# The S5 input product of a hybrid mixer block, issued for two row bands at a time (QB = 1 to 2)

## The chip, the core and the metric

One core of one Trainium2 chip runs the whole program: TensorE (matmuls into PSUM), VectorE, ScalarE, GpSimd and SyncE, with DMA engines that load the weights. The metric is the device time of one execution in microseconds.

## The reference, cut to what matters

One layer over 256 tokens of width 2048: a mixer of three branches (gated delta rule, gated linear attention, S5 state space), then cross attention, then a convolutional feed-forward part. The change is in the S5 branch:

```python
def s5_ssm(u, lam_re, lam_im, log_step, b_re, b_im, c_re, c_im, d_skip):
    uf = u.astype(f32).reshape(bsz, s, S5_GROUPS, S5_GROUP)      # 64 groups of 16 features
    ...
    bbr = zr[..., None] * br - zi[..., None] * bi                # discretised input matrices
    bbi = zr[..., None] * bi + zi[..., None] * br
    bu_r = jnp.einsum('bsgh,gph->sbgp', uf, bbr)                 # the input product: 16 -> 64 a group
    bu_i = jnp.einsum('bsgh,gph->sbgp', uf, bbi)
    ...
    _, _, xr, xi = lax.associative_scan(combine, (a_r, a_i, bu_r, bu_i), axis=0)   # over 256 tokens
    y = (jnp.einsum('sbgp,ghp->bsgh', xr, c_re) - jnp.einsum('sbgp,ghp->bsgh', xi, c_im))
    ...
```

All of it is float32.

## The kernel before

**The large products.** Weights come in slabs of two k-tiles by 512 columns (`raw`, loaded through SyncE's queue). `load_w` (L206) splits each into a high part `whi` (ScalarE's cast) and a low part `wlo` (VectorE's subtraction). TensorE multiplies high and low parts in separate passes: `tile_passes` (L222 high, L226 low) where features come out on the partitions, `proj_tok` (L282, L286) where tokens do. Those passes use all 128 rows of the array. The order of high and low passes in `tile_passes` is the same in both kernels. Their sums stand in five PSUM tiles `acc`; the other three PSUM banks are a ring of tiles `mx` (L126), which every small product shares.

**Background work.** The three branches are generators. `proj` and `proj_tok` call `pump` after each slab, which lets each generator run for as much as its rate allows; a `yield` says what the step was worth. So the small products stand among the slabs' passes. A scheduler with a timeline of its own then orders the instructions of each engine; after that every engine works in that order.

**The S5 generator** (`s5_core`). For each half of the sequence (128 tokens) it fills `X`, the input product for all 64 groups, real and imaginary, with two groups of 64 states on the 128 partitions. The input `su` has 32 rows (two groups of 16 features) for each product, so a feature tile holds four row bands of 32, and `Bl` holds the matrices for the same rows. One step takes one band `q` and two feature tiles: four matmuls (L921: two feature tiles by real and imaginary) into one `mx` tile, each 32 rows by 128 weight columns by 128 tokens at `tile_position=(32 * q, 0)`, and then one copy of that tile to `X` on ScalarE (L925). There are 16 steps in a half. When the last is copied, the scan runs on VectorE, three small instructions for each token (L931 to L933), and then the output product (L946). The first half's steps stand among the passes of the delta rule's key slabs (L222, L226), where the key tiles are also transposed (L397); the second half's among the last gate and value slabs (L282, L286) and the first delta-rule output gate slabs (L222, L226). L593 is a product of the delta rule's state, in 64-row bands that alternate between two `mx` tiles; L602, L599 and L640 are others of it.

The constant `QB` sets how many bands one step takes. The loop is

```python
            for f2 in range(4):
                for q2 in range(0, 4, QB):
                    pss = [self.mx([P, 2, 2, P]) for _ in range(QB)]
                    for n in range(2):
                        ft = 2 * f2 + n
                        for c in range(2):
                            for q, ps in enumerate(pss, q2):
                                rs = slice(32 * q, 32 * q + 32)
                                nc.tensor.matmul(ps[:, n, c, :], self.Bl[c][rs, ft, :], su[rs, ft, tk], start=True,
                                                 stop=True, tile_position=(32 * q, 0))
                    for q, ps in enumerate(pss, q2):
                        p0 = 8 * f2 + q
                        nc.scalar.copy(X[:, :, p0:p0 + 5:4, :].rearrange("p c n s -> p n c s"), ps)
                    yield 1.0 * QB
```

Of the kernel before, what the change touches and what calls it, by code (L numbers as in the profile page):

```python
# [40 lines left out]
R_EB = 0.4  # L41
SP5 = 0
TAIL = 3
QB = 1
HPA = 0
R_N1 = 0.8
R_N2 = 1.3
# [41 lines left out]
class Net:  # L89
# [814 lines left out]
    def s5_core(self, ctr, cti):  # L904
# [5 lines left out]
        for hf in range(2):  # L910
            X = self.s5p.tile([P, 2, 32, P], F32, name="X", tag="X")
            tk = slice(hf * P, hf * P + P)
# [4 lines that stand above are left out]
# [6 lines left out]
# [4 lines that stand above are left out]
            for t in range(P):  # L927
# [645 lines left out]
```

## Time and profile before

| | |
|---|---|
| median of 3 runs | 1924.62 us (1921.52 to 1929.48) |
| the profiled execution | 1925.81 us |
| its span, first to last instruction | 1924.0 us |
| mean granted TensorE clock | 0.991 |
| DMA | 363.93 MB, mean 189 GB/s |

The profile gives each engine's busy time; the chain of work that ended last, which follows the last instruction back through whatever released it, and so tells which engine sets the end; and groups of instructions by line, with what ended the idle time ahead of them. In a group's row, `32*128 32x128` is a weight tile of 32 rows by 128 columns and 32 rows by 128 moved columns. "PEclk" in a table by stage is the clock granted to TensorE as a share of full speed. Matmuls are pipelined: the busy time of one overlaps the next, so that a mean duration is longer than the distance from one to the next.

### The profile page before, as it was taken

The page shows a single profiled execution, that of the slowest core. Times are in us where ns is not written, and L with a number is a line of the kernel's source. Part 1 is how long each engine was busy: PE and PEld are TensorE (multiplying, and loading weights), DVE is VectorE, ACT ScalarE, POOL GpSimd, SP SyncE. Part 2 cuts the span into 40 slices and gives each one's busy share as a digit, 9 for nine tenths or more (in the row PEclk, how much of TensorE's full clock was granted, in tenths as well). Part 3 has the DMA queues.
Part 4 walks back from the last instruction along what each step waited for, and adds up shares of the span by engine and source line. Part 5 has one row for each costly group of instructions (what it writes and reads, how often), then busy time and mean ns, then how long its engine had stood idle before and what let it go on. Part 6 is the DMA issues. An engine that isn't in the chain of part 4 may idle for free.

```text
span 1924.0 us, 28133 instructions
## 1 busy us (share of the span) xinstructions
PE 1873.0 (97%) x10440; PEld 1573.9 (82%) x10440; DVE 1415.4 (74%) x2719; ACT 959.6 (50%) x1428; POOL 67.4 (4%) x117
## 2 busy tenths in 40 slices
PE   7999999999999999999999997999999999999997
PEld 6788888777877688888888986888888888888886
DVE  6878999997469999977666755777666677644445
ACT  5655544443564444444455654655555555544442
POOL 0000012020000000000000000000000000000000
PEclk9989999999999999999999998999999999999999
DMA  7544477674445575666587544766666656766664
GB/s 256 164 130 155 155 210 234 195 253 140 133 121 162 182 225 177 213 216 216 186 266 225 174 153 140 219 182 184 201 188 188 189 183 186 228 215 198 198 195 131
DMA packets 107482, 363.93 MB, mean 189 GB/s; under 512 B 12320, under 2 KB 20896, under 8 KB 106832
## 3 DMA queue, kind: packets, MB, share of 16 engines
q1 hardware_dynamic: 97696, 328.32, 55.3%
q0 software_dynamic: 9648, 33.81, 5.3%
q8 instruction: 82, 1.34, 0.3%
q14 instruction: 56, 0.46, 0.1%
HBM read 350.47 MB, written 11.61 MB: 188 GB/s over the span
## 4 chain that ended last, share of the span: by engine, by line
PE 89%; DVE 6%; ACT 2%; issue 1%; DMA 1%; DVEq 0%; SPq 0%; POOL 0%; ACTq 0%; POOLq 0%
PE acc L282 28%; PE acc L222 27%; PE acc L286 14%; PE acc L226 14%; DVE wlo L206 2%; PE mx L921 2%; DMA raw<-in 1%; ACT whi L206 1%; DVE r L388 1%; PE mx L183 0%; PE mx L640 0%; DVE mm L931 0%; DVE f L518 0%; PE mx L946 0%; DVE X L933 0%
## 5 line engine op out<-in xcount | busy, mean ns | idle before, releaser
L206 DVE TENSOR_TENSOR wlo<-raw,whi 128x1024 fp32r<-128x1024 f32 (+1 forms) x632 | 752.3, 1195 | 388.3 <-ACT whi L206 366.6
L206 ACT CAST whi<-raw 128x1024 fp32r<-128x1024 f32 (+1 forms) x632 | 645.6, 1029 | 672.1 <-PE acc L282 339.1
L222 PE MATMUL acc<-aa,whi 128*128 128x512 f32 x2224 | 620.7, 398 | 10.7 <-DVE r L212 8.3
L222 PEld LDWEIGHTS acc<-aa,whi 128*128 128x128 f32 x2224 | 383.6, 190 | 63.9 <-issue 9.8
L226 PEld LDWEIGHTS acc<-aa,wlo 128*128 128x128 f32 x2224 | 345.4, 191 | 59.1 <-DVE wlo L206 11.5
L226 PE MATMUL acc<-aa,wlo 128*128 128x256 f32 x2224 | 362.1, 283 | 7.6 <-DVE wlo L206 7.4
L282 PE MATMUL acc<-whi,aa 128*128 128x512 f32 (+1 forms) x1408 | 346.5, 383 | 0.0
L282 PEld LDWEIGHTS acc<-whi,aa 128*128 128x128 f32 x1408 | 255.3, 188 | 53.3 <-issue 2.3
L286 PE MATMUL acc<-wlo,aa 128*128 128x512 f32 (+1 forms) x704 | 191.5, 383 | 2.8 <-DVE wlo L206 2.7
L286 PEld LDWEIGHTS acc<-wlo,aa 128*128 128x128 f32 x704 | 127.9, 188 | 31.5 <-DVE wlo L206 6.6
L282 PE MATMUL acc<-whi,ach 128*128 128x512 f32 x352 | 137.0, 389 | 0.0
L282 PE MATMUL acc<-whi,acl 128*128 128x512 f32 x352 | 136.9, 389 | 0.0
L931 DVE TENSOR_TENSOR mm<-M,X 128x128 f32<-128x128 f32 x254 | 98.7, 389 | 5.1 <-ACT X L925 0.3
L286 PE MATMUL acc<-wlo,ach 128*128 128x512 f32 x352 | 95.4, 389 | 0.0
L282 PEld LDWEIGHTS acc<-whi,ach 128*128 128x128 f32 x352 | 66.1, 188 | 13.7
L286 PEld LDWEIGHTS acc<-wlo,ach 128*128 128x128 f32 x352 | 66.1, 188 | 13.7
L282 PEld LDWEIGHTS acc<-whi,acl 128*128 128x128 f32 x352 | 66.0, 188 | 13.7
L933 DVE TENSOR_TENSOR X<-X,s__868 128x64 f32<-128x64 f32 x255 | 71.6, 281 | 4.8
L282 PE MATMUL acc<-whi,mgx 128*128 128x512 f32 x256 | 64.3, 391 | 0.1
L211 ACT COPY r<-acc 128x256 f32<-128x256 f32 x143 | 49.6, 362 | 27.3 <-PE acc L222 26.8
L932 DVE TENSOR_TENSOR s__868<-mm 128x64 f32<-128x64 f32 x255 | 56.5, 222 | 4.5
L212 DVE TENSOR_TENSOR r<-r,acc 128x256 f32<-128x256 f32 x143 | 57.0, 413 | 0.9 <-ACT r L211 0.9
(439 smaller groups left out, 1558.5 us busy)
## 6 DMA issues: line engine op xcount, KB each, us to landing
raw<-in SPq DMA_DIRECT2D x600, 512.0 KB, 4.0
raw<-in SPq DMA_DIRECT2D x32, 256.0 KB, 2.7
gd<-r POOLq DMA_DIRECT2D x24, 256.0 KB, 4.4
f<-gd POOLq DMA_DIRECT2D x12, 512.0 KB, 4.8
f<-Rd POOLq DMA_DIRECT2D x4, 512.0 KB, 7.2
f<-in POOLq DMA_DIRECT2D x4, 512.0 KB, 4.5
gp<-in POOLq DMA_DIRECT2D x8, 256.0 KB, 4.7
xn<-in POOLq DMA_DIRECT2D x1, 2048.0 KB, 11.0
```

The source lines that it names most:

```text
L206: self.last = (nc.scalar.copy(hi, raw), self.seq(lambda: nc.vector.tensor_sub(lo, raw, hi.bitcast(F32))))
L211: self.nc.scalar.copy(r, acc[:, T:2 * T])
L212: self.nc.vector.tensor_add(r, r, acc[:, 0:T])
L222: nc.tensor.matmul(accs[m], hi[:, kk, ms[m]], xs[kk].rearrange("p c s -> p (c s)"), start=ks[kk] == 0, stop=ks[kk] == KT - 1)
L226: nc.tensor.matmul(accs[m][:, :T], lo[:, kk, ms[m]], xs[kk][:, 0, :], start=False, stop=False)
L282: nc.tensor.matmul(accs[t], xs[kk][i][:, t * P:(t + 1) * P], hi[:, kk, :], start=ks[kk] == 0 and i == 0, stop=False)
L286: last[:] = [nc.tensor.matmul(accs[t], xs[kk][0][:, t * P:(t + 1) * P], lo[:, kk, :], start=False, stop=ks[kk] == KT - 1)]
L388: nc.vector.scalar_tensor_tensor(c[:, d:], raw[:, :T - d], w[:, j, 3 - d:4 - d], c[:, d:], op0=ALU.mult, op1=ALU.add)
L921: nc.tensor.matmul(ps[:, n, c, :], self.Bl[c][rs, ft, :], su[rs, ft, tk], start=True, stop=True, tile_position=(32 * q, 0))
L931: nc.vector.tensor_mul(m, self.M, prev[:, None].broadcast_to([P, 2, 2, 32]))
L932: nc.vector.tensor_add(s, m[:, :, 0, :], m[:, :, 1, :])
L933: nc.vector.tensor_add(X[:, :, :, t], X[:, :, :, t], s)
```

## The change

One constant:

```diff
-QB = 1
+QB = 2
```

One step of `s5_core` now takes two `mx` tiles and two bands. For each feature tile and each of the real and imaginary parts it issues the matmul of the one band and then that of the other, so that neighbours have different rows of the array and different PSUM tiles; then both tiles are copied, and the step counts 2.0 instead of 1.0. There are 8 steps in a half.

TensorE, second half, among the gate slabs. `mx_4924` is the step's PSUM tile, `bl0` and `bl1` are the real and imaginary matrices. Before:

```order
L286 MATMUL acc_4821<-wlo_4908,aa_448 128x512 x2
L921 MATMUL mx_4924<-f8_107,bl0_449 128x128
L921 MATMUL mx_4924<-f8_107,bl1_450 128x128
L921 MATMUL mx_4924<-f8_107,bl0_449 128x128
L921 MATMUL mx_4924<-f8_107,bl1_450 128x128
L282 MATMUL acc_4820<-whi_4931,aa_448 128x512 x4
L282 MATMUL acc_4821<-whi_4931,aa_448 128x512 x4
L286 MATMUL acc_4820<-wlo_4932,aa_448 128x512 x2
L286 MATMUL acc_4821<-wlo_4932,aa_448 128x512 x2
L921 MATMUL mx_4948<-f8_107,bl0_449 128x128
```

Now:

```order
L286 MATMUL acc_4821<-wlo_4908,aa_448 128x512 x2
L921 MATMUL mx_4924<-f8_107,bl0_449 128x128
L921 MATMUL mx_4925<-f8_107,bl0_449 128x128
L921 MATMUL mx_4924<-f8_107,bl1_450 128x128
L921 MATMUL mx_4925<-f8_107,bl1_450 128x128
```

The same four rows follow once more for the second feature tile, and then L282. What stood behind the next slab (`mx_4948`) is now the second tile here. Six of the eight steps of the second half read like this. The first two of it do not alternate throughout; the first, behind the output product of the first half:

```order
L946 MATMUL mx_4645<-X_869,f4_4468 32x128 x4
L921 MATMUL mx_4778<-f8_107,bl0_449 128x128
L921 MATMUL mx_4778<-f8_107,bl1_450 128x128
L921 MATMUL mx_4778<-f8_107,bl0_449 128x128
L921 MATMUL mx_4779<-f8_107,bl0_449 128x128
L921 MATMUL mx_4779<-f8_107,bl1_450 128x128
L921 MATMUL mx_4779<-f8_107,bl0_449 128x128
L921 MATMUL mx_4778<-f8_107,bl1_450 128x128
L921 MATMUL mx_4779<-f8_107,bl1_450 128x128
```

Three matmuls of one band are followed by three of the other, and then one of each. In the first half the steps stand closer, and the scheduler takes some of them apart. The second step there, `mx_926` and `mx_927`, now:

```order
L921 MATMUL mx_871<-f8_107,bl1_450 128x128
L921 MATMUL mx_926<-f8_107,bl0_449 128x128
L921 MATMUL mx_926<-f8_107,bl1_450 128x128
L921 MATMUL mx_926<-f8_107,bl0_449 128x128
L921 MATMUL mx_926<-f8_107,bl1_450 128x128
L226 MATMUL acc_1404<-aa_448,wlo_1466 128x256 x2
L222 MATMUL acc_1405<-aa_448,whi_1409 128x512 x2
```

`mx_926` stands behind the first pair (whose last matmul is the first row), and `mx_927` comes 14 large passes later, with the third pair right behind it. Two more pairs of the first half are taken apart in this way. By the order, the first half's 16 tiles stand in 10 places among the large passes before and in 8 now; the second half's in 15 before and in 8 now. In the first half, four more L222 matmuls stand ahead of the last tile's than before.

ScalarE, second half, copies of `X` among the weight casts. Before:

```order
L206 CAST whi_4973<-raw_4972 128x1024
L925 COPY X_4777<-mx_4924 128x2x2x128
L206 CAST whi_5003<-raw_5002 128x1024
L925 COPY X_4777<-mx_4948 128x2x2x128
L206 CAST whi_5027<-raw_5026 128x1024
```

Now:

```order
L206 CAST whi_4973<-raw_4972 128x1024
L925 COPY X_4777<-mx_4924 128x2x2x128
L925 COPY X_4777<-mx_4925 128x2x2x128
L206 CAST whi_5009<-raw_5008 128x1024
L206 CAST whi_5027<-raw_5026 128x1024
```

The two copies of a step now stand together, ahead of the casts. The order of the queues of SyncE and GpSimd is the same in both kernels.

## Prediction

> **What bounds the kernel now.** I read the page's busy lines first, then the chain of work that ended last, then the group of the line that is changed.
>
> ```profile
> PE 1873.0 (97%) x10440; PEld 1573.9 (82%) x10440; DVE 1415.4 (74%) x2719; ACT 959.6 (50%) x1428; POOL 67.4 (4%) x117
> PE 89%; DVE 6%; ACT 2%; issue 1%; DMA 1%; DVEq 0%; SPq 0%; POOL 0%; ACTq 0%; POOLq 0%
> PE acc L282 28%; PE acc L222 27%; PE acc L286 14%; PE acc L226 14%; DVE wlo L206 2%; PE mx L921 2%; DMA raw<-in 1%; ACT whi L206 1%; DVE r L388 1%; PE mx L183 0%; PE mx L640 0%; DVE mm L931 0%; DVE f L518 0%; PE mx L946 0%; DVE X L933 0%
> L921 PE MATMUL mx<-f,bl 32*128 32x128 f32 x256 | 35.6, 299 | 0.2 <-DVE bl L897 0.2
> ```
>
> TensorE is the bound: 89% of the chain. Line 921, the S5 input product, is 2% of it, so some 38 us at the very most. The program has 128 such matmuls and the trace 256 records: each fp32 matmul runs as two passes of 32 rows by 128 columns. The busy time is not the price, since passes overlap in it; the price has to be read from the chain in order of time, stage by stage. L921 stands in two stages, one for each half of the sequence:
>
> ```profile
> core 0: us, PE busy (x) PEld busy (x) DVE busy (x) ACT busy (x) POOL busy (x), PEclk, DMA share, GB/s
> 120.40:134.00 13.60, 13.60 (x54) 11.62 (x53) 6.84 (x24) 6.64 (x14) 0.00 (x0) 0.50 0.17 55
> 134.00:158.70 24.70, 24.70 (x169) 20.90 (x169) 13.59 (x38) 14.14 (x23) 0.00 (x0) 1.00 0.34 107
> 158.70:450.00 291.30, 283.55 (x1626) 232.86 (x1626) 281.81 (x646) 132.94 (x182) 32.01 (x55) 1.00 0.65 198
> 484.00:558.00 74.00, 74.00 (x401) 59.46 (x391) 36.33 (x56) 43.49 (x62) 0.53 (x1) 1.00 0.45 136
> 558.00:580.00 22.00, 17.43 (x151) 14.72 (x149) 22.00 (x37) 11.85 (x15) 0.00 (x0) 1.00 0.40 120
> ```
>
> In 120.4 to 158.7 (first half) and 484 to 558 (second half) TensorE is busy without a gap while VectorE has half its time free; DMA is far from full. What TensorE saves there moves the end of the stage. In the stages behind (158.7 to 450, 558 to 580) VectorE is the full engine: 281.8 of 291.3 us, and 22.0 of 22.0. They begin when the scan of L931 has the last X tile, so they begin earlier by what the loading stage saves, and don't shrink. The first row also shows 13.6 us at half the clock, at a place where L921 stands.
>
> **The price of a group now.** The chain in order of time, second half, and behind it three stretches from elsewhere (the first half's later groups, and L593):
>
> ```profile
> 484.60 1.82 PE mx L921 x15
> ...
> 493.10 2.04 PE acc L282 x8
> 495.13 0.91 PE acc L286 x4
> 496.04 1.81 PE acc L282 x8
> 497.85 0.91 PE acc L286 x4
> 498.76 1.08 PE mx L921 x8
> 499.84 2.04 PE acc L282 x8
> 501.88 0.91 PE acc L286 x4
> 502.78 1.08 PE mx L921 x8
> ```
>
> ```profile
> 135.65 2.19 PE mx L921 x24
> ...
> 139.91 1.08 PE mx L921 x8
> ...
> 153.93 1.64 PE mx L921 x16
> ...
> 428.12 1.09 PE mx L593 x16
> ```
>
> A lone group (4 matmuls, 8 passes, one row band) takes 1.08 us, and the eight L282 matmuls behind it take 2.04 instead of 1.81: 0.23 us for the switch between 32-row and full tiles. Where two or three groups of different bands happen to stand together, the next one adds only 1.64 − 1.08 = 0.56 (2.19 − 1.64 = 0.55): the bands already overlap, by a lookahead of a few passes. L593 is the nearest thing to what the change makes: fp32, 128 weight columns, 128 moved columns, two bands (of 64 rows) in turn, each with its own PSUM bank. Its 16 passes take 1.09 us, what 8 passes of one band take. So a pair whose bands alternate should take 1.09, against 2 × (1.08 + 0.23) apart or 1.64 + 0.23 side by side.
>
> **Second half, step by step.** Before: 15 clusters by the order, the first of two groups (1.82), then 14 lone ones: 1.82 + 14 × 1.08 + 15 × 0.23 = 20.4 us. After: 8 clusters. Six alternate at every matmul: 6 × 1.09. The first two go three matmuls of one band, three of the other, then one each; between 1.09 (full overlap) and 1.64 (only the lookahead) I take 1.4. Sum 6 × 1.09 + 2 × 1.4 + 8 × 0.23 = 11.2. Saved 9.2.
>
> **First half.** Before: 10 clusters of 24, 8, 8, 24, 8, 16, 8, 8, 16 and 8 passes, at full clock 2 × 2.19 + 6 × 1.08 + 2 × 1.64 + 10 × 0.23 = 16.4. After: 8 clusters, and not all pairs: three PSUM tiles are not enough for the density here, and the order tears three pairs apart. One is an alternating pair with a lone band behind it (1.09 + 0.56 = 1.65); two are a lone band, then a pair that alternates only in its second half (between 1.65 and 2.19, I take 1.8, nearer the overlapped end since all three bands differ); two are full pairs (1.09); three are lone (1.08). 1.65 + 2 × 1.8 + 2 × 1.09 + 3 × 1.08 + 8 × 0.23 = 12.5. Saved 3.9, of which 0.9 is lost again for the scan, because the order puts four more L222 matmuls (0.23 each, as 1.81 / 8 shows for the like L282) in front of the last lone band. Net 3.0. That some of these ran at half clock changes nothing as long as the half-clock stretch keeps its length: the work that is pushed out of it is then other work.
>
> **What else moves.** The X copies of L925 come two in a row on ScalarE, with the weight casts behind them by 0.6 us more:
>
> ```profile
> L925 ACT COPY X<-mx x32: 566/587/632, 120.4 to 559.3; 128x512 f32<-128x512 f32 x32
> PEld mx L921 <- ACT X L925: 0.2, 1, 0.2
> ```
>
> Two copies are 1.17 us. The casts feed three buffers and ScalarE is busy 43.5 of 74 us in the second half, so I cost this at nothing; if that cover went, TensorE would wait at the next L282. Each pair now holds two of the three mx tiles from its first matmul to the second copy. Before, TensorE waited 0.2 us for that in the whole first half. From below it costs 0, from above one copy, 0.59 us, at each of the 16 pairs, 9.4 us; I take 0, nearest the 0.2, since pairs of the second half stand at least 12 matmuls (2.7 us, 1.81 + 0.91) apart. SP's and POOL's queues keep their order; VectorE's rows around the scan change places within some 20 rows, with the same work in each stage.
>
> **Sum.** 9.2 + 3.0 = 12.2 us. The profiled execution took 1925.81 us (span 1924.0), 1.2 above the median of 1924.62; it goes to 1913.6, the median to 1912.4. I say 1912. About 0.5% (9.6 us) is what a measurement of this kernel tells from no change: the three runs shown lie 8 us apart.
>
> **A rule weighed.** Here is the pass-to-pass time, from one lone group shown whole and one cut by the window's edge after seven passes:
>
> ```profile
> 498.69 1.15 PE L921 MATMUL mx<-f,bl 32*128 32x128 f32 x8
> ...
> 502.71 1.04 PE L921 MATMUL mx<-f,bl 32*128 32x128 f32 x7
> ```
>
> One pass of a band takes 0.11 us, so a neighbouring group that adds 0.56 has three of its eight passes under the group before it. The Trainium skill (TensorE: Matmul & The Clock Gate, Part 3: Packing small matmuls — row/col tiling) says that row groups overlap, but that matmuls start and end strictly in program order. By strict order a group behind another could hide one pass alone and would add 0.77; the torn pairs would then cost about 1 us more in all, and the sum would be 11. The trace's 0.56 says that a later band does run ahead, so I keep my prices.
>
> **Rivals.**
> - The bands don't alternate, or not at this size: 32-row bands in turn gain no more than neighbours do. For it: no row shows 32-row bands that alternate by the matmul. Against: L593 and the 0.56. Pairs at 1.64 and the torn clusters at 2.19: second half 8 × 1.64 + 1.84 = 15.0, saved 5.4; first half 3 × 2.19 + 2 × 1.64 + 3 × 1.08 + 1.84 = 14.9, saved 1.5, net 0.6. Sum 6, time 1918.6.
> - VectorE takes back the first half. It is full from 158.7 to 450; if its stage there is tied to weights arriving and not to X, only the 9.2 of the second half stay: 1915.4. If the second half too is lost to the 22 us behind it (TensorE stands idle 4.6 there), up to that much again: 1920. For it: VectorE's full rows. Against: both stages open with work that waits for X.
> - The half-clock stretch changes. 13.6 us at 0.50 cost 6.8. With less 32-row work in it, it could end sooner; without it the time is 1912.4 − 6.8 = 1905.6, and a longer one costs half of what it adds. The Trainium skill (the same page, Part 1: The HAM clock gate) has the full clock back after one busy window of about 3.4 us; the row at 0.50 has TensorE busy for four such stretches, so the trace doesn't bear that out, and I can't foretell this length.
> - Slower: TensorE, which issues in order, stands at a pair's first matmul of the second band until ScalarE has freed its mx tile, with every accumulating matmul behind it. The price is ScalarE's place: a copy (0.59) behind a weight cast (1.03 mean) is 1.6 us. From 12.2 / 16 = 0.76 us a pair the gain is gone; with 1.6 at all 16 pairs, 25.9 − 12.2 = 13.7 is lost and the time is 1938. Against it: the 0.2 us. The Trainium skill (TensorEngine Tiling (Array Packing), PSUM Bottleneck) warns of this: tiling speeds TensorE, and the copies out of PSUM may become the bottleneck; copies of 1.17 for a pair of 1.09 would agree with it if pairs followed each other, which they do only in the first half.
>
> ```profile
> L206 ACT CAST whi<-raw 128x1024 fp32r<-128x1024 f32 (+1 forms) x632 | 645.6, 1029 | 672.1 <-PE acc L282 339.1
> ```
>
> **How the numbers follow.** The forecast (1908 to 1917 with its unknown prices) has 0.62; no alternation or VectorE taking part back (1915 to 1921) 0.22; the half-clock stretch shorter (1904 to 1909) 0.10; slower or unchanged by PSUM waits 0.06. The range 1905 to 1921 leaves out about 2 in 10. Faster than 1915.0: 0.54 of the first case and all of the third, 0.64. Within 0.5%: the rest of the first, the second, 0.02 of the last, 0.32. Slower: 0.04.
>
> **What would show it.** In the chain of the changed kernel, L921 pieces of 16 passes at about 1.09, eight clusters in the second half, and that half's loading stage 9 us shorter than 74. Pieces of 1.6 for a pair would show the alternation wrong; TensorE waiting for X of L925 by more than a few us would show the PSUM rival; a stage 158.7 to 450 that is longer by what was saved ahead of it, the VectorE one. A granted clock at half for longer or shorter than 13.6 us near 120 would be the third. It would be wrong altogether if the pairs fall apart on the chip, or if VectorE starts its scan no earlier.

## The result and the profile after

| | before | changed |
|---|---|---|
| median, first comparison | 1924.62 us (7 runs, 1921.52 to 1929.48) | 1915.03 us (7 runs, 1911.12 to 1919.79) |
| ratio | | 0.9944 [0.9932, 0.9956] |
| median, second comparison | 1923.43 us (16 runs) | 1911.23 us (6 runs) |
| ratio | | 0.9941 [0.9929, 0.9953] |
| profiled execution, span, granted clock | 1925.81, 1924.0, 0.991 | 1911.12, 1909.3, 0.994 |

The kernel became 0.56 to 0.59% faster, some 11 us, just past the 0.5% that can be told from no change. For the second comparison I had expected 1914 to 1916, and it came out 3 us lower. The page of the changed kernel (busy lines, the chain by engine and by line, the group of L921):

```profile
PE 1857.7 (97%) x10440; PEld 1561.2 (82%) x10440; DVE 1414.6 (74%) x2719; ACT 958.1 (50%) x1428; POOL 67.4 (4%) x117
PE 86%; DVE 8%; issue 2%; ACT 2%; DMA 1%; DVEq 0%; SPq 0%; POOL 0%; ACTq 0%; POOLq 0%
L921 PE MATMUL mx<-f,bl 32*128 32x128 f32 x256 | 21.3, 283 | 0.2 <-DVE bl L897 0.2
```

TensorE's busy time fell by 15.3 us, L921's by 14.3 (35.6 to 21.3), with the same 256 records. VectorE's share of the chain rose from 6 to 8%: the first sign that part of the saving met another path. The chain in order of time, first half, then second half:

```profile
123.90 1.65 PE mx L921 x23
128.75 1.08 PE mx L921 x8
132.12 1.65 PE mx L921 x23
137.48 1.09 PE mx L921 x16
143.10 1.09 PE mx L921 x16
145.81 1.08 PE mx L921 x8
148.01 1.08 PE mx L921 x8
```

```profile
474.38 1.82 PE mx L921 x16
480.32 1.42 PE mx L921 x16
487.67 1.09 PE mx L921 x16
488.76 2.04 PE acc L282 x8
490.79 0.91 PE acc L286 x4
...
497.14 1.09 PE mx L921 x16
503.89 1.09 PE mx L921 x16
513.37 1.09 PE mx L921 x16
522.84 1.09 PE mx L921 x16
```

A pair whose bands alternate takes 1.09 us, what one band takes alone, and the switch back to full tiles costs the same 0.23 (2.04 against 1.81). The stages, cut at the same instructions in both kernels. Before: from the start of the first half's products to the last X copy, from the second half's first L921 to the first L673, and from there to the first L640:

```profile
core 0: us, PE busy (x) PEld busy (x) DVE busy (x) ACT busy (x) POOL busy (x), PEclk, DMA share, GB/s
119.00:158.70 39.70, 39.54 (x234) 33.75 (x234) 21.83 (x63) 21.49 (x39) 0.00 (x0) 0.83 0.30 94
484.50:543.10 58.60, 58.60 (x298) 46.68 (x294) 26.41 (x43) 31.60 (x46) 0.53 (x1) 1.00 0.46 137
543.10:583.80 40.70, 35.76 (x245) 29.93 (x244) 35.08 (x60) 25.47 (x36) 0.00 (x0) 0.97 0.38 114
```

The same three in the changed kernel:

```profile
119.00:149.80 30.80, 30.50 (x238) 25.69 (x238) 21.76 (x63) 21.24 (x39) 0.00 (x0) 1.00 0.44 130
474.30:526.80 52.50, 52.50 (x306) 42.55 (x302) 26.52 (x43) 32.02 (x47) 0.53 (x1) 1.00 0.52 153
526.80:567.60 40.80, 36.36 (x239) 29.34 (x238) 34.30 (x58) 23.67 (x34) 0.00 (x0) 0.92 0.37 114
```

The first stage is 8.9 us shorter; 0.17 × 39.7 = 6.7 of that is clock, since the stretch at half speed is gone, and 2.2 is work. The second is 6.1 shorter at full clock. The third is as long as before; its lower clock (0.92 against 0.97) does not show in its length. The shift between the two traces is 10.2 us where the second half begins (484.5 to 474.3), 16.2 at L640 (583.8 to 567.6) and 14.7 at the end of the span. The 1.5 given back on the way differs from profile to profile (between -0.4 and 3.1 us in the other kernels below, against the same profile of before), and I attribute it to nothing.

### The profile page after: what moved, and what is told of

Read it like the earlier page. It is cut to its first block, busy times and chain, and to the rows that moved or that the text cites. A ratio compares the mean times of both kernels' runs of the same rounds, so it can differ in the third digit from the quotient of the medians.

```text
span 1909.3 us, 28128 instructions
## 1 busy us (share of the span) xinstructions
PE 1857.7 (97%) x10440; PEld 1561.2 (82%) x10440; DVE 1414.6 (74%) x2719; ACT 958.1 (50%) x1428; POOL 67.4 (4%) x117
## 4 chain that ended last, share of the span: by engine, by line
PE 86%; DVE 8%; issue 2%; ACT 2%; DMA 1%; DVEq 0%; SPq 0%; POOL 0%; ACTq 0%; POOLq 0%
PE acc L282 27%; PE acc L222 26%; PE acc L286 14%; PE acc L226 13%; DVE wlo L206 3%; DMA raw<-in 1%; PE mx L921 1%; DVE mm L931 1%; DVE r L388 1%; PE mx L183 1%; ACT whi L206 1%; PE mx L640 1%; DVE X L933 0%; DVE f L518 0%; PE mx L946 0%
## 5 line engine op out<-in xcount | busy, mean ns | idle before, releaser
L222 PE MATMUL acc<-aa,whi 128*128 128x512 f32 x2224 | 620.1, 398 | 9.3 <-DVE r L212 6.9
L222 PEld LDWEIGHTS acc<-aa,whi 128*128 128x128 f32 x2224 | 383.8, 190 | 62.8 <-issue 8.8
L226 PEld LDWEIGHTS acc<-aa,wlo 128*128 128x128 f32 x2224 | 344.9, 191 | 60.4 <-DVE wlo L206 13.4
L282 PE MATMUL acc<-whi,aa 128*128 128x512 f32 (+1 forms) x1408 | 345.4, 382 | 0.0
L282 PEld LDWEIGHTS acc<-whi,aa 128*128 128x128 f32 x1408 | 255.8, 188 | 52.3 <-issue 1.6
L282 PE MATMUL acc<-whi,ach 128*128 128x512 f32 x352 | 136.9, 389 | 0.0
L282 PE MATMUL acc<-whi,acl 128*128 128x512 f32 x352 | 136.9, 389 | 0.0
L282 PEld LDWEIGHTS acc<-whi,ach 128*128 128x128 f32 x352 | 66.1, 188 | 13.7
L286 PEld LDWEIGHTS acc<-wlo,ach 128*128 128x128 f32 x352 | 66.1, 188 | 13.7
L282 PEld LDWEIGHTS acc<-whi,acl 128*128 128x128 f32 x352 | 66.0, 188 | 13.7
L282 PE MATMUL acc<-whi,mgx 128*128 128x512 f32 x256 | 64.4, 391 | 0.8 <-ACT whi L206 0.8
```

Source lines behind the costliest of these rows:

```text
L222: nc.tensor.matmul(accs[m], hi[:, kk, ms[m]], xs[kk].rearrange("p c s -> p (c s)"), start=ks[kk] == 0, stop=ks[kk] == KT - 1)
L226: nc.tensor.matmul(accs[m][:, :T], lo[:, kk, ms[m]], xs[kk][:, 0, :], start=False, stop=False)
L282: nc.tensor.matmul(accs[t], xs[kk][i][:, t * P:(t + 1) * P], hi[:, kk, :], start=ks[kk] == 0 and i == 0, stop=False)
L286: last[:] = [nc.tensor.matmul(accs[t], xs[kk][0][:, t * P:(t + 1) * P], lo[:, kk, :], start=False, stop=ks[kk] == KT - 1)]
```

## How small differences were separated from the clock

A mean granted clock that is 0.001 lower goes with 1.9 us of a span of 1920, and runs of one kernel differ by several thousandths. So beside the ratio, each kernel has two more numbers below: what it lost to the clock, (1 − granted clock) × span, averaged over its runs, and its net time, the time less that. Over 68 runs the kernel before lost 16.0 us, and its net time was 1908.1 to 1908.4 in three comparisons. "±" is a standard error.

The net time is an index and not exact. TensorE's last matmul ends 12 us before the span does, and in every profile the clock falls to half behind it: 4.5 to 5.7 us of each loss stand there and cost nothing. That part is much the same in all kernels and falls out of differences. Over the 167 runs whose clock is on record, 1 us more lost goes with 0.85 us more time within a kernel, so that taking off the whole loss is slightly too much: by 0.85 the change's work below would be 8.8 us and not 8.4.

| kernel (runs) | median us | ratio | lost to the clock | net |
|---|---|---|---|---|
| the change (7) | 1915.03 | 0.9944 [0.9932, 0.9956] | 14.5 | 1900.4 ± 0.5 |
| the change again (6) | 1911.23 | 0.9941 [0.9929, 0.9953] | 12.4 | 1899.2 ± 0.3 |
| one band, then the other (12) | 1922.88 | 0.9995 [0.9982, 1.0008] | 17.9 | 1904.8 ± 0.6 |
| second half only (12) | 1918.69 | 0.9978 [0.9967, 0.9989] | 17.1 | 1902.1 ± 0.4 |
| first half only (12) | 1918.25 | 0.9974 [0.9964, 0.9984] | 12.5 | 1906.2 ± 0.6 |
| four bands, second half (6) | 1911.73 | 0.9940 [0.9923, 0.9958] | 13.4 | 1899.2 ± 0.5 |
| four bands, both halves (5) | 1928.59 | 1.0033 [1.0021, 1.0045] | 27.8 | 1901.5 ± 0.8 (too low, see its experiment) |
| last pair five times (8) | 1917.99 | 0.9974 [0.9963, 0.9986] | 15.1 | 1903.5 ± 0.3 |
| fourth pair five times (8) | 1917.48 | 0.9975 [0.9964, 0.9986] | 15.1 | 1902.6 ± 0.5 |
| last two pairs only (12) | 1926.10 | 1.0003 [0.9990, 1.0015] | 18.1 | 1908.1 ± 0.4 |
| first two pairs only (11) | 1920.54 | 0.9974 [0.9961, 0.9987] | 12.7 | 1908.0 ± 0.4 |

## The experiments

**Grouping without alternation.** Two bands a step, but one band's four matmuls and then the other's:

```diff
-                    for n in range(2):
-                        ft = 2 * f2 + n
-                        for c in range(2):
-                            for q, ps in enumerate(pss, q2):
-                                rs = slice(32 * q, 32 * q + 32)
+                    for q, ps in enumerate(pss, q2):
+                        rs = slice(32 * q, 32 * q + 32)
+                        for n in range(2):
+                            ft = 2 * f2 + n
+                            for c in range(2):
```

> Two bands a step as in the change, but all four matmuls of the one band, then all four of the other: the grouping without the alternation. If alternation is what saves, second-half pieces of 16 passes take 1.64 us in the chain and not 1.09; the second half saves 8 x 1.64 + 8 x 0.23 against 20.4, so 5.4 us, the first half (10 clusters, as before) nothing; time 1919 to 1921, between the two kernels. If fewer tile switches are all that matters, pieces and time are those of the change (1915). If bands ran strictly in program order, pieces would be 1.85 and the time 1921 to 1922. If the half-clock stretch near 120 us depends on the alternation, it is back here (13 us at 0.50).

The chain of this kernel, second half:

```profile
497.48 1.64 PE mx L921 x16
499.12 2.04 PE acc L282 x8
```

A pair takes 1.64, as two neighbours do before the change; the alternation is what makes it 1.09. The second half's loading stage was 55.4 us, 3.2 shorter than before and 2.9 longer than in the changed kernel. Net it gained 3.5, and the clock took 2.7 more than from the kernel before in the same comparison (17.9 against 15.2), so that the ratio is 0.9995. The 2.7 has a standard error of 1.2. The median, 1922.9, is above the 1919 to 1921 that the first case of the expectation gave, and the stretch at half clock near 120 us is back, at 6.8 us and not 13.

**Each half alone.**

```diff
-QB = 2
+QB = (1, 2)   # second half only; (2, 1): first half only
+                qb = QB[hf]
```

The loop and its `yield` then go by `qb`, here and in the kernels below that set it.

> Two bands a step in the second half of the sequence only, one in the first. Net of the clock the second half moved the trace by 7.7 us: time 1917, the shift at 110 to 480 us zero. Rival (the gain is the half-clock stretch near 120 us, which the alternation in the first half removes): that stretch is here as before, and the time is 6.8 us above the change plus the 3.0 of the first half, about 1925.

> Two bands a step in the first half only. TensorE time alone: 3.0 us off, time 1921 to 1922. Rival (the first half's alternation removes the half-clock stretch for good): 3.0 + 6.8 = 9.8 off, time 1915, and no stretch at 0.50 near 120 us.

Net, the second half gave 6.2 (1908.3 to 1902.1), the first 2.1 (to 1906.2); together 8.3, and the whole change 7.9 and 9.1 in its two comparisons. The halves add up. Both medians miss what was expected: 1918.7 against 1917 for the second half, and 1918.3, between 1921 to 1922 and the rival's 1915, for the first. The first half's time fell by 0.26%, some 5 us, more than twice its net gain: it lost 2.7 less to the clock than the kernel before did beside it (15.2). The 13.6 us near 120 us, second half only, then first half only:

```profile
120.40:134.00 13.60, 13.60 (x83) 11.74 (x82) 8.46 (x30) 7.08 (x16) 0.00 (x0) 0.75 0.21 71
```

```profile
120.40:134.00 13.60, 13.46 (x108) 11.45 (x107) 10.31 (x31) 10.88 (x22) 0.00 (x0) 1.00 0.21 59
```

Where lone groups stand there, half of the stretch runs at half clock (mean 0.75); where pairs alternate, none does.

**What the last pairs are worth.** In the changed kernel the last pair of the second half stands behind the first L673. To see whether its length counts, its matmuls were issued five times; and, to compare, those of the fourth pair, in the middle of the loading stage. The four repetitions write the same values again.

```diff
+                            for r in range(5 if (hf, f2, q2) == (1, 3, 2) else 1):   # (1, 1, 2): fourth pair
-                            for q, ps in enumerate(pss, q2):
+                              for q, ps in enumerate(pss, q2):
```

> The changed kernel with the matmuls of the second half's last pair (behind the small gate product) issued five times over, same results: 64 more passes, 32 steps of 0.11, so 3.6 us more on TensorE at that place. If the saving of the last clusters was lost because VectorE's and ScalarE's chain sets the end there, this costs 0 to 1 us against the changed kernel. If TensorE's time counts there as everywhere, 3.6.

> The same 64 passes more, but at the second half's fourth pair, among the gate slabs, where the chain is TensorE's: 3.6 us over the changed kernel under both theories. It prices the other one.

The fourth pair behaved as expected: the loading stage was 3.6 us longer (56.1 against 52.5), the net time 3.4 above that of the change in the same comparison (1902.6 against 1899.2). The last pair cost 4.3 (1903.5), more than either case of its expectation (0 to 1, or 3.6). But this run doesn't answer the question. ScalarE's timeline behind that pair:

```profile
542.64 4.67 ACT L704 ACTIVATE f<-f 128x1024 f32<-128x1024 f32 x4 [1.10 <-DVE f L702]
547.21 1.05 ACT L926 COPY X<-mx 128x512 f32<-128x512 f32 x2
```

The scheduler, which counted the longer pair, put its copies behind L704, so that they began at 547.2, ten us later than in the changed kernel (537.7). Making a step longer moved other work with it, and isn't the mirror of making it shorter. So the saving itself was tried alone, in the last two pairs of the second half only:

```diff
-QB = 2
+QB = 1
+                qb = 2 if (hf, f2) == (1, 3) else 1
```

> The kernel before, with two bands a step only in the last two steps of the second half: the same lone groups up to the small gate product L673, then one pair behind it where three lone groups stood. On TensorE that is 2 x 1.31 = 2.6 us less. If the end of that stage is set by the chain of ScalarE and VectorE behind L673, the time is that of the kernel before (within 1 us), and the distance from the first L673 to the first L640 is 39.5 to 41 us as in all kernels. If TensorE's time counts there, 2.6 us less and a distance of 37 to 38.

By the prediction's prices this saves 2.6. It saved nothing: ratio 1.0003, net 1908.1 as before. Its loading stage and the one behind it:

```profile
482.00:540.70 58.70, 58.70 (x307) 46.73 (x303) 26.40 (x43) 32.59 (x47) 0.53 (x1) 1.00 0.46 137
540.70:582.30 41.60, 36.14 (x239) 29.35 (x238) 35.73 (x64) 24.36 (x35) 0.00 (x0) 0.92 0.37 111
```

From L673 to L640 it took 41.6, against 40.7 before with three lone groups there and 40.8 in the changed kernel with one pair. What sets this stretch is in the chain of the changed kernel:

```profile
526.92 1.06 PE mx L673 x4
...
529.46 3.01 PE acc L222 x7
...
533.44 1.06 ACT f L681
...
535.81 1.07 ACT f L682
...
538.05 1.22 DVE wlo L206
539.26 2.35 DVE f L688 x4
...
542.29 0.68 DVE f L702
```

The chain leaves TensorE behind L673 and goes over ScalarE (L681, L682) to VectorE's L688 and L702. Before, it stayed on TensorE until 565.6 and only then went to VectorE. The path over ScalarE and VectorE is as long as it was: L688 begins 11.4 us behind the first L673 before and 12.3 now. The last X tile is ready 16.7 us behind the first L673 before and 11.9 now, and the first L640 stands 40.7 and 40.8 behind it. So neither a shorter TensorE nor an earlier X is worth anything there. The other profiles agree. With three lone groups behind L673 the distance to L640 is 39.5 to 40.7 us (three kernels), with a pair 39.5 to 41.6 (six), with none 39.5 and 41.4 (the two kernels with four bands); only the last pair issued five times gives more, 46.2.

**The clock alone.** Alternation in the first step of the first half, the first two pairs, and nowhere else:

```diff
-QB = 2
+QB = 1
+                qb = 2 if (hf, f2) == (0, 0) else 1
```

> The kernel before, with two bands a step only in the first two steps of the first half. On TensorE the first place is 1.65 instead of 2.19, some 0.5 us. If it is the density of the first S5 matmuls behind VectorE's pause that keeps the clock up near 120 us, there is no half-clock stretch there, and the runs lose 2 to 3 us less to the clock than those of the kernel before: 1920 to 1921. If the later steps matter as much, the stretch stays and the time is 1922.5 to 1923.5.

The same stretch near 120 us, here and in the kernel with the last two pairs only:

```profile
120.40:134.00 13.60, 13.46 (x101) 11.34 (x96) 10.47 (x34) 10.44 (x23) 0.00 (x0) 1.00 0.21 69
```

```profile
120.40:134.00 13.60, 13.60 (x83) 11.68 (x82) 8.49 (x32) 6.81 (x15) 0.00 (x0) 0.75 0.17 56
```

The net time is that of the kernel before (1908.0), and still it is 0.26% faster, 5 us: all of it is clock, 12.7 lost instead of 17.8 beside it. These matmuls save no work that counts and remove the stretch at half clock that stood there. A shorter one follows in this kernel, 3.4 us where lone bands stand again and TensorE is busy throughout:

```profile
135.80:139.20 3.40, 3.40 (x9) 2.72 (x10) 2.58 (x4) 0.97 (x3) 0.00 (x0) 0.51 0.81 264
```

Over all profiles, the stretch at the opening of the first half stands in the four kernels that don't alternate there (13.7 us before, 6.8 in the three others) and in none of the seven whose first half opens with alternating pairs (the kernel with four bands in both halves has another placement, below). In those four the clock falls 1.2 to 1.8 us behind the first L921, while the first three groups still run (where they alternate, they end after 1.65 us). Up to the end of these groups TensorE's order is the same in all eleven kernels but for the alternation, and its wait for VectorE just ahead is 0.65 to 1.30 us in the four and 0.52 to 1.08 in the seven. So neither another place nor another wait tells the two kinds apart; the alternation does. Runs say the same more weakly: those without alternation there lost 17.7 us to the clock (36 runs; the kernel before 16.0 over 68), those with it 13.6 (58 runs, from 12.4 for the change again to 15.1 for the two with repeated pairs).

**Four bands.** Two more PSUM tiles are taken from the large products' pool (`acc`), so that all four bands of a step alternate; in the second half only, and then in both:

```diff
-QB = 2
+QB = (2, 4)   # (4, 4) in the second kernel
+                qb = QB[hf]
-                    pss = [self.mx([P, 2, 2, P]) for _ in range(QB)]
+                    pss = [self.mx([P, 2, 2, P]) if i < 2 else self.ps_acc.tile([P, 512], F32, name="acc", tag="acc").rearrange("p (n c s) -> p n c s", n=2, c=2) for i in range(qb)]
```

> Two bands a step in the first half, four in the second (two tiles from mx, two from the ring of accumulators). If four bands overlap as two do, whole steps of 32 passes take about 1.1 us in the chain, and the second half costs TensorE 8.9 us instead of 11.6: up to 2.7 us under the change, 1912 to 1915; VectorE's chain from 530 us on can take that back to zero (1915). If only two bands run at a time, steps of 32 take 2.0 and the time is 1915 to 1916. If the accumulators' ring is what is short, TensorE waits for it and the time is over 1917.

> Four bands a step in both halves, two tiles of mx and two of the accumulators' ring. Its first half stands in six places instead of eight, and the first eight products stand ahead of the first key slab's end. If four bands overlap fully everywhere the first half saves up to 4 us more than the change: 1908 to 1912. If the first step, which now waits for the discretised matrices in TensorE's order, holds the accumulating matmuls up, or the ring of five accumulators is short where a projection needs four, the time is 1915 to 1925.

Second half only: TensorE's timeline at one step, from its first matmul to the next large one, is

```profile
509.48 0.38 PE L922 MATMUL mx<-f,bl 32*128 32x128 f32 x2
509.49 0.38 PE L922 MATMUL acc<-f,bl 32*128 32x128 f32 x2
...
510.37 0.28 PE L922 MATMUL acc<-f,bl 32*128 32x128 f32 x2
510.58 2.11 PE L282 MATMUL acc<-whi,aa 128*128 128x512 f32 x8
```

32 passes in 510.58 − 509.48 = 1.10 us, what 8 passes of one band take. The time is that of the change (0.9940, net 1899.2). By the expectation TensorE was to save up to 2.7 more (8.9 against 11.6), and none of it shows in the net time of six runs. The scheduler takes the first steps apart: the second half's products stand in seven places, against eight in the change, and not in four. The last step now stands ahead of L673, where its length does count. This profile also has 6.8 us at half clock from 471.6, where no other has any. Why the rest does not show is open: the two tiles taken from the large products may cost what the steps save.

In both halves it became slower, by 0.33%: 1928.6, above both cases of the expectation. The waits of that kernel have a row of 20.8 us that is 0.2 in the kernel before, and in the stage before the first half the clock fell; the two rows by stage are up to the first L922 and from there on:

```profile
PE mx L922 <- DVE bl L897: 20.8, 1, 20.8
```

```profile
94.50:112.70 18.20, 0.00 (x0) 0.00 (x0) 13.09 (x21) 4.45 (x10) 2.65 (x4) 0.50 0.34 90
112.70:121.80 9.10, 9.08 (x79) 8.28 (x80) 2.46 (x11) 5.01 (x10) 0.00 (x0) 0.50 0.01 2
```

Its first S5 step stands ahead of other products in TensorE's order, and TensorE waits 20.8 us for VectorE's B matrices. The granted clock is 0.50 for 27.3 us, 13.7 of the 27.8 lost by the measure above. But TensorE had nothing to do in 18.2 of them, where a low clock costs nothing; only the 9.1 busy us behind cost some 4.5. So 9.1 too much is taken off here, and the net time of 1901.5 should read about 1910.6, which is no better than before and points to the wait, more than to the clock, as what makes this kernel slow. No kernel tried is clearly faster than the change.

## Why the prediction was right, and where its sum was off

The forecast of 1912 from 1905 to 1921 holds the 1915.0 and the 1911.2, and the sign is right. Its sum, 12.2, came out at some 11 by two errors of opposite sign, so that its closeness is partly luck: TensorE's work gave 8.4 (the mean of the change's 13 runs, net), and the clock gave 2.5 that the sum didn't have (13.5 lost in those runs, 16.0 before).

- *A pair costs 1.09, the switch 0.23:* 1.09 and 0.23 in the trace, and it is the alternation that does it (1.64 without). The first rival, no gain beyond neighbours, is what the kernel without alternation is; it had 6 us, and gave 3.5 net.
- *Second half 9.2:* mis-sized; 6.1 in the trace, 6.2 net in the kernel with this half alone. Of the 3.0 missing, 0.4 is in the first two pairs, 1.82 + 1.42 against 2 × 1.4. The other 2.6 is the step that counted all 15 clusters on TensorE's path: three lone groups stand behind L673, where the path over ScalarE and VectorE sets the end, and turning them into a pair gave 0 ± 0.5. That is the second rival, VectorE taking back, in the stretch that it named, at 2.6 of the up to 4.6 that it allowed there. What would have told it ahead: the row 558 to 580 with VectorE busy 22.0 of 22.0 and TensorE idle for 4.6 was priced as a stage that begins as soon as X is there, though by the chain above it hangs on L673. So the sign that the prediction named, a loading stage 9 us shorter than 74, did come (from the first L921 to the end of the last it is 72.8 before and 63.2 now), and still only 6.1 of it counted.
- *First half 3.0 net:* 2.2 in the trace and 2.1 ± 0.6 net. The two later clusters of 24 passes took 1.65 where I took 1.8, so by my own terms it should have been 3.3. The trace doesn't show where the other 1.1 is: what lies at half clock before can't be read at full clock to that precision. What was saved stayed saved: VectorE didn't take the first half back.
- *The half-clock stretch keeps its length:* wrong. It is gone, as in the third rival: 6.8 us in the profiled execution and 2.5 on average. It had 0.10; the range reached to it only in part. That the alternation in the first two pairs removes it at that place is shown; what in it does so is not. TensorE is as busy in both cases (13.46 and 13.60 of 13.60), so busy time alone doesn't tell the two apart. The Trainium skill (TensorE: Matmul & The Clock Gate, Part 1: The HAM clock gate) has the clock follow how busy TensorE was in the window before; by the busy time of these rows the clock would be the same in both.
- *X copies at nothing:* held. The changed kernel's waits from 119 to 160 have one row for it, 0.4 us in all, and those of the second half (474 to 540) have none, so the slower rival fell:

```profile
PEld mx L921 <- ACT X L925: 0.4, 1, 0.4
```

- *The rule weighed:* by it a neighbouring group would add 0.77. The pairs at 1.64 without alternation bear out the 0.56 of the trace before.

Left open: whether two bands that alternate in one PSUM bank would do the same was not tried, so what the two banks contribute isn't known.

## What to carry over

Where a product uses 32 of TensorE's 128 rows, let neighbouring matmuls use different row bands and PSUM tiles: a second band then costs nothing (1.09 against 1.08), while bands that merely stand side by side overlap by three passes of eight. Price each place by the chain that ends the stage there, not by the engine that is full on the whole: 6.1 us came from the stretch that TensorE sets and none from the same edit 20 us later. When a change is worth half a per cent, compare times net of the granted clock as well, and run a part of the change that moves the clock and no work; here that told 8.4 us of work from 2.5 of clock. Look where the low clock stands, though: where TensorE has nothing to do it costs nothing.

## What was not expected of the hardware

- Four 32-row bands that alternate run 32 fp32 passes of 128 columns in 1.10 us, within 0.02 of the 1.08 for 8 passes of one band.
- Whether the first two pairs (32 passes, 2.2 us of matmuls) alternate decides whether 6.8 to 13.7 us at the opening of a stage run at half the clock: the granted clock of 120.4 to 134.0 is 0.50 and 0.75 without, 1.00 with, and TensorE is busy for at least 13.46 of 13.60 us either way.
- Behind a wait of 20.8 us at the head of TensorE's order the clock stayed at 0.50 for 9.1 us of matmuls without a gap.
